# Gated attention's first pair beside the later projections, latent conditioning moved to routing and to the second attention

## The chip, the core and the metric

The kernel runs on one core of a Trainium2 chip. The metric is the device time of one execution in microseconds; lower is better. The names of the engines are those of the profile: PE is TensorE (matmuls, with PEld for its weight loads), DVE is VectorE, ACT is ScalarE, POOL is GpSimd, SP is SyncE, whose queue issues most of the DMAs.

## The reference, cut to what matters

Two transformer blocks run one after the other on 512 tokens of width 1024. The first block has 16 meta tokens in front (528 in all):

```
xn = rmsnorm(h); proj = xn @ w_in              # dq dk dv gq gk gv gr zf zb
da = diff_attention(dq, dk, dv)                # 4 heads, two softmaxes each, rope
log_g = log_sigmoid(z @ gate_w2 + b) / 16      # forward and backward gates
go = gla_bidirectional(gq, gk, gv, log_g)      # 4 heads, gated linear attention
go = rmsnorm(go) * silu(gr)
h = h + concat([da, go]) @ w_out
hn = rmsnorm(h)
h = h + peer_ffn(hn)                           # top-16 of 16384 experts, 8 heads
x = rmsnorm(h)
```

The second block is conditioned by a vector `c` (for the latents `x`) and a vector `c_ctx` (for 256 context tokens):

```
mod   = silu(c)     @ ada_w + ada_b            # 6 x 1024: sh1 sc1 g1 sh2 sc2 g2
mod_c = silu(c_ctx) @ ada_w[:, :2048] + ada_b  # only the first two
k_ctx, v_ctx = modulate(rms_norm(ctx), mod_c) @ w_in
x = x + g1 * (mix(modulate(rms_norm(x), sh1, sc1)) @ w_out)   # fourier, conv, attention
x = x + g2 * mlp(modulate(rms_norm(x), sh2, sc2))
```

## The kernel before, in words

Matrix products are made from fp32r halves: a weight tile of 128x1024 is loaded by SP (512 KB), ACT casts its high half, DVE or POOL subtracts to get the low half (`wsplit`, lines 232 to 242), and three matmuls (`mm3`, lines 220 to 223) stand for one product. The Tile scheduler puts the instructions of an engine in order: by when they are expected to be ready, and among those by their place in the program; parts inside `manual_schedule` keep the program's order.

**Projections** (lines 303 to 533). `order` lists 16 column tiles of `w_in` (0 to 3 dq, 4 to 7 dk, 8 to 11 gq and gk, 12 to 15 gr), `z` and two values `v0` (dv) and `v1` (gv). `projT`, `projz` and `projV` make them, with weights fetched four ahead into three buffers. PSUM has two double banks `psA` and four single ones `psB`; dq, gr and the values use `psB`. Postponed work (`rotate` for rope, `gate` for the gates) is held in `later` and goes out one projection later. Beside this, `ada_steps` makes the conditioning: `ada_w` is streamed as 48 rows of 128x1024, and one DVE instruction with an accumulator (line 322) multiplies a row with `silu(c)` and sums it; the first 16 rows are also summed against `silu(c_ctx)`, so there are 64 such instructions. Each projection asks for one row (`ada_go`), `projV` for two per chunk.

**Attentions** (lines 534 to 833). `gla_all` is a generator of 26 steps, 13 for each pair of heads: a diagonal, nine levels (s = 1 to 256: two exps and two masked copies on ACT, two multiplies on DVE, two adds on POOL, then the products of the level before on PE), the rest of the products, the meta rows, and at last the output matmuls with the head norm. `da_all` has 19 steps for the softmax attention. The loop at line 821 takes one gated step and about 19/22 of a softmax step at a time. Before it, an ACT table with exp and ln is loaded by hand after the last `Silu`. When the softmax steps end, three tiles of `w_out` are fetched.

**Routing** (lines 1018 to 1103) makes 16 query tiles `pq` (24 matmuls of 512 columns each), the scores, and the top 16 on DVE (`max`, `max_index`, `match_replace`); after every second tile `route` combines them. Beside it `ahead` runs passes over the expert table `u` (`upass`: 24 matmuls of 384 columns), one after an even and two after an odd tile, 24 in all; their low halves are made by POOL. `NR` = 29 passes lie before the **spread** stage, which starts when DVE has the gates; `NG` = 56 passes lie before the **v stage**, and their results are stored to DRAM and read back. In the v stage the first 56 steps have `v` alone, the other 72 also a `u` pass.

**Second attention** (lines 1598 to 1725). `pipe` runs 32 steps; step i makes the scores of one head and block, the transposes of step i-2 and the output of step i-3, with conv and Fourier steps aside in the first half. The output projection after it reads `mod[:, 16:]`.

```
821        for t in range(26):
822            next(gla, None)
823            while done < NDA and done * NE < NDA * (t + 1):
824                next(da, None)
```

## Time and profile before

| what | value |
|---|---|
| median of 3 runs | 2335.8 us (2331.62 to 2337.16) |
| the profiled execution | 2333.9 us, its span 2332.1 us |
| PE busy | 2237.0 us, 96% |
| DVE busy | 1729.0 us, 74% |
| ACT busy | 1006.2 us, 43% |
| POOL busy | 623.6 us, 27% |

The page gives busy times over the whole span. A share of the span mixes stages with different limits, so the view by stretches is read beside it: it gives each engine's busy time in a stage. Matmuls are pipelined and a row's mean duration is longer than the distance between two of them; where the pace matters, the start times of the timeline are used.

### The profile page before, as it was taken

What the parts mean: (1) busy time and instruction counts of PE and PEld (TensorE: products, weight loads), DVE (VectorE), ACT (ScalarE), POOL (GpSimd) and SP (SyncE); (2) the same over time, 40 slices, a digit from 0 to 9 for tenths busy, and PEclk for the clock granted to TensorE, in tenths of its full rate; (3) what the DMA queues carried; (4) which work ended last, traced back from release to release, by engine and by line L of the source; (5) the groups of instructions that cost most, each with busy time, mean ns of one, the idle gap of its engine ahead of it and who ended that gap; (6) DMA issues with size and microseconds to landing.
All of it is one profiled execution on the core that took longest, in us unless ns stands there. A gap on an engine that the chain in (4) does not pass through costs nothing.

```text
span 2332.1 us, 31023 instructions
## 1 busy us (share of the span) xinstructions
PE 2237.0 (96%) x11457; PEld 1883.3 (81%) x11457; DVE 1729.0 (74%) x3188; ACT 1006.2 (43%) x1439; POOL 623.6 (27%) x418
## 2 busy tenths in 40 slices
PE   7999898999999999999999999999998999999997
PEld 6777466899889878889999999999776777888885
DVE  8997776799999778887777887878687566433434
ACT  5337774433378733333333333333443654322322
POOL 2123213344310122223343443343372022000001
PEclk9999999999999999999999999999999999999999
DMA  7760023433267799998999998999321221322320
GB/s 248 261 224 10 1 81 137 167 128 111 93 231 286 304 346 340 339 335 314 312 333 314 316 335 311 322 329 310 110 93 66 73 80 64 125 92 82 117 82 36
DMA packets 158151, 458.00 MB, mean 196 GB/s; under 512 B 15248, under 2 KB 61968, under 8 KB 155696
## 3 DMA queue, kind: packets, MB, share of 16 engines
q1 hardware_dynamic: 120800, 319.57, 38.7%
q0 software_dynamic: 37200, 136.46, 16.9%
q8 instruction: 89, 1.46, 0.2%
q14 instruction: 62, 0.51, 0.1%
HBM read 419.80 MB, written 36.18 MB: 196 GB/s over the span
## 4 chain that ended last, share of the span: by engine, by line
PE 76%; DVE 8%; issue 2%; ACT 1%; DMA 1%; POOL 1%; DVEq 0%; SPq 0%; POOLq 0%; ACTq 0%
PE pu L221 8%; PE po L222 7%; PE po L221 7%; PE po L223 7%; PE pu L222 7%; PE pu L223 7%; PE pm L222 2%; PE pm L223 2%; PE pa L221 2%; PE pm L221 2%; PE pa L222 2%; DVE ac L1516 2%; PE pa L223 2%; PE pq L1187 2%; PE psB L221 2%
## 5 line engine op out<-in xcount | busy, mean ns | idle before, releaser
L221 PE MATMUL pu<-hn,uhi 128*128 128x384 f32 x1024 | 356.9, 348 | 1.6 <-DVE kc L932 0.9
L223 PE MATMUL pu<-hn,ulo 128*128 128x384 f32 x1024 | 347.2, 339 | 4.6 <-DVE ulo L234 2.7
L222 PE MATMUL pu<-hn,uhi 128*128 128x384 f32 x1024 | 347.5, 339 | 0.0
L221 PE MATMUL po<-vhi,ch 128*128 128x512 f32 x768 | 301.7, 393 | 4.8 <-ACT ch L1308 4.8
L222 PE MATMUL po<-vlo,ch 128*128 128x512 f32 x768 | 301.6, 393 | 0.1
L223 PE MATMUL po<-vhi,cl 128*128 128x512 f32 x768 | 299.2, 390 | 0.0
L1200 POOL DMA_INDIRECT gr<-in_u,idx x128 | 144.6, 1130 | 448.5 <-DVE aact L1205 416.7
L233 ACT CAST whi<-wraw 128x1024 fp32r<-128x1024 f32 x104 | 108.8, 1049 | 333.0 <-PE pm L222 127.8
L1297 ACT CAST vhi<-vraw 128x1024 fp32r<-128x1024 f32 x128 | 134.7, 1053 | 250.5 <-PE po L223 138.9
L234 POOL TENSOR_TENSOR wlo<-wraw,whi 128x1024 fp32r<-128x1024 f32 x52 | 131.6, 2536 | 383.6 <-ACT whi L233 330.1
L233 ACT CAST uhi<-uraw 128x1024 fp32r<-128x1024 f32 x105 | 110.1, 1048 | 270.0 <-PE pu L222 241.3
L1200 POOL DMA_INDIRECT gr<-in_v,idx x128 | 156.7, 1225 | 226.7 <-DVE acc L1214 189.1
L221 PEld LDWEIGHTS pu<-hn,uhi 128*128 128x128 f32 x1024 | 192.9, 188 | 5.6 <-ACT uhi L233 2.1
L223 PEld LDWEIGHTS pu<-hn,ulo 128*128 128x128 f32 x1024 | 192.7, 188 | 5.5 <-DVE ulo L234 3.1
L222 PEld LDWEIGHTS pu<-hn,uhi 128*128 128x128 f32 x1024 | 193.1, 189 | 3.5
L1309 DVE TENSOR_TENSOR vlo<-vraw,vhi 128x1024 fp32r<-128x1024 f32 x128 | 156.3, 1221 | 50.6 <-ACT vhi L1297 45.0
L234 DVE TENSOR_TENSOR wlo<-wraw,whi 128x1024 fp32r<-128x1024 f32 x52 | 63.6, 1222 | 161.5 <-ACT whi L233 161.2
L221 PEld LDWEIGHTS po<-vhi,ch 128*128 128x128 f32 x768 | 144.8, 189 | 33.9 <-ACT ch L1308 5.3
L223 PEld LDWEIGHTS po<-vhi,cl 128*128 128x128 f32 x768 | 144.9, 189 | 31.7 <-DVE cl L1310 0.2
L222 PEld LDWEIGHTS po<-vlo,ch 128*128 128x128 f32 x768 | 144.8, 189 | 27.7 <-DVE vlo L1309 0.6
L1214 DVE SCALAR_TENSOR_TENSOR acc<-gr,aact,acc 128x1024 f32<-128x1024 f32 x126 | 154.5, 1279 | 0.0
L1205 DVE CUSTOM_DVE_ANT_0 gr<-gr,hnat 128x1024 f32<-128x1024 f32 x128 | 152.6, 1220 | 0.0
(584 smaller groups left out, 5074.6 us busy)
## 6 DMA issues: line engine op xcount, KB each, us to landing
uraw<-in_ut SPq DMA_DIRECT2D x129, 512.0 KB
vraw<-in_v SPq DMA_DIRECT2D x128, 512.0 KB
aw<-in_ada SPq DMA_DIRECT2D x48, 512.0 KB
gt<-gd SPq DMA_DIRECT2D x42, 480.0 KB
wraw<-in_m SPq DMA_DIRECT2D x32, 512.0 KB
xraw<-in_m SPq DMA_DIRECT2D x32, 512.0 KB
gd<-gs SPq DMA_DIRECT2D x6, 2048.0 KB
sd<-ge SPq DMA_DIRECT2D x56, 192.0 KB
```

Of the source, the lines that this page charges most:

```text
L221: PE.matmul(out, lhs[0], rhs[0], start=first, stop=False)
L222: PE.matmul(out, lhs[0], rhs[1], start=False, stop=False)
L223: PE.matmul(out, lhs[1], rhs[0], start=False, stop=last)
L233: S.copy(hi, raw)
L234: eng.tensor_sub(lo, raw, hi.bitcast(F32))
L1187: PE.matmul(pv[:, q], oa[:, q0 + q], ob[:, j, q0 + q], start=j == 0, stop=j == 1)
L1200: G.indirect_dma_start(r, None, src, bass.IndirectOffsetOnAxis(ap=idx[:, j:j + 1], axis=0))
L1205: V.tensor_tensor_reduce(out=r, in0=r, in1=hnat, scale=1.0, scalar=0.0, op0=OP.mult, op1=OP.add, accum_out=aact[:, j:j + 1])
L1214: V.scalar_tensor_tensor(A, r, aact[:, j:j + 1], A, op0=OP.mult, op1=OP.add)
L1297: S.copy(wh, raw)
L1309: V.tensor_sub(wl, raw, wh.bitcast(F32))
L1516: V.scalar_tensor_tensor(ac[:, t], cv[:, t, j:j + N], w, ac[:, t], op0=OP.mult, op1=OP.add)
```

## The change: what it does

It reorders the projections so that the gated attention's inputs (`z`, 8 to 11) come first; the other 15 entries follow, and 12 of the 26 gated steps are emitted between their parts. dq, gr and the values move to `psA`; `psB` holds the gated steps and the values' meta rows. Weights have two buffers and are fetched two ahead, all low halves are made by DVE, `t1` has one buffer. `gr` gets one `Silu` at tile 15, and the table load by hand goes. Only the 16 context rows of the conditioning stay with the projections. The first 16 rows for the latents go to the routing (one per query tile), the other 32 to the second attention (one per step); `silu(c)` is computed in the routing, stored to DRAM and read again. `ahead` makes 7 passes in 4 tiles where it made 6, `NR` goes to 33 and `NG` to 60. The softmax steps are spread over 12 of the remaining 14 gated steps.

```
-    NR = 29
-    NG = 56
+    NR = 33
+    NG = 60
-    order = [0, 1, 'z', 8, 9, 10, 11, 'v1', 2, 3, 4, 5, 6, 7, 12, 13, 14, 15, 'v0']
-    NT = 18
+    order = ['z', 8, 9, 10, 11, 0, 1, 2, 3, 4, 5, 6, 7, 'v1', 12, 13, 14, 15, 'v0']
+    NT = 5
...
-            for j in range(48):
-                w = adp.tile([128, D], F32, name="aw", bufs=4)
+            for j in range(16):
+                w = adp.tile([128, D], F32, name="aw", bufs=2)
...
-                eng = G if len(srcs) % 3 == 0 and len(srcs) < 22 else V
-                ready.append(wsplit(wp, src, n, bufs=bufs, tag=tag, rbufs=bufs, eng=eng))
+                ready.append(wsplit(zp if tag == "wz" else wp, src, n, bufs=bufs, tag=tag, rbufs=bufs))
-            while len(ready) < 4:
+            while len(ready) < 2:
...
-                p = psB()
+                p = psA()[:, 0]
...
-                silu.append(S.activation(gr[:, j - 12], gr[:, j - 12], AF.Silu))
+                if j == 15:
+                    S.activation(gr, gr, AF.Silu)
...
         def projV(j, dst):
-            pp = [psB() for _ in range(4)] + [psA()[:, 0]]
+            pa = [psA() for _ in range(2)]
+            pp = [pa[t // 2][:, t % 2] for t in range(4)]
...
         gla = gla_all()
+        GS = 12
+        steps, parts = 0, 0
+        rest = 8 + 4 + 4 + 4
         for o in order[NT:]:
+            for _ in proj(o):
+                parts += 1
+                while steps < GS and steps * rest < GS * parts:
+                    next(gla)
+                    steps += 1
...
+    def ada_row(pool, j, sil, bufs):
+        w = pool.tile([128, D], F32, name="aw", bufs=bufs)
+        nc.sync.dma_start(w, a['ada'][j])
+        V.tensor_tensor_reduce(out=w, in0=w, in1=sil, scale=1.0, scalar=0.0, op0=OP.mult, op1=OP.add,
+                               accum_out=mod[:, j:j + 1])
...
-        NDA, NE = 19, 22
+        NDA, NE = 19, 12
-        with tc.issue_after(ins_of(silu[-1])):
-            table = S.preload_act_table_set("natural_log_exp_and_others")
-        for t in range(26):
+        for t in range(26 - GS):
...
+        sil = wp.tile([128, D], F32, name="sil")
+        nc.sync.dma_start(sil, bass.AP(tensor=a['cv'].tensor, offset=a['cv'].offset, ap=[[0, 128], [1, 1024]]))
+        S.activation(sil, sil, AF.Silu)
+        nc.sync.dma_start(sild, sil)
...
-            ahead(1 + j % 2)
+            ada_row(wp, j, sil, 3)
+            ahead(1 if j % 4 == 2 else 2)
             if j % 2:
                 route(j // 2)
+        ada_done(0, 16)
+        gains(0)
...
+        def cond(i):
+            if i < 32:
+                ada_row(adp, 16 + i, sil, 3)
-        pipe(32, (aside, 0), (na_scores, 0), (na_turn, 2), (na_out, 3))
+        pipe(32, (aside, 0), (na_scores, 0), (na_turn, 2), (na_out, 3), (cond, 0))
+    ada_done(16, 48)
+    gains(2)
```

`ada_done` adds the bias to a range of `mod`, `gains` makes one of the three scale vectors; both are one or two DVE instructions of a few columns.

## Rows read from the trace of the kernel before

**Rows 1.** The page, parts 1 and 5: busy time by engine; one group of instructions

```profile
PE 2237.0 (96%) x11457; PEld 1883.3 (81%) x11457; DVE 1729.0 (74%) x3188; ACT 1006.2 (43%) x1439; POOL 623.6 (27%) x418
...
L1205 DVE CUSTOM_DVE_ANT_0 gr<-gr,hnat 128x1024 f32<-128x1024 f32 x128 | 152.6, 1220 | 0.0
```

**Rows 2.** Busy time by stretch: length, PE, PEld, DVE, ACT, POOL, PEclk, DMA share, GB/s

```profile
24.70:189.50 164.80, 156.69 (x869) 128.83 (x868) 156.65 (x253) 59.91 (x79) 36.10 (x18) 0.99 0.62 217
189.50:313.00 123.50, 108.94 (x550) 71.69 (x550) 102.24 (x180) 100.74 (x198) 37.56 (x29) 0.96 0.02 5
313.00:338.00 25.00, 22.70 (x84) 12.65 (x83) 12.61 (x14) 19.78 (x35) 2.42 (x2) 1.00 0.07 23
...
418.00:441.00 23.00, 22.87 (x119) 20.36 (x120) 11.10 (x37) 9.95 (x13) 1.84 (x1) 1.00 0.69 251
441.00:615.00 174.00, 174.00 (x913) 157.13 (x912) 171.80 (x833) 55.74 (x79) 80.58 (x34) 1.00 0.34 115
...
845.00:1045.00 200.00, 200.00 (x884) 165.62 (x883) 162.21 (x291) 71.78 (x98) 43.31 (x46) 1.00 0.95 336
1045.00:1640.00 595.00, 595.00 (x2987) 541.71 (x2986) 473.47 (x629) 214.88 (x286) 236.29 (x193) 1.00 0.91 317
...
1802.00:1856.00 54.00, 51.99 (x275) 36.02 (x275) 31.30 (x70) 36.37 (x64) 0.00 (x0) 0.97 0.16 51
1856.00:1906.00 50.00, 49.47 (x356) 39.79 (x354) 33.23 (x81) 30.28 (x66) 6.28 (x3) 1.00 0.31 101
```

**Rows 3.** Timeline of PE in the projections: start us, length, what, idle before

```profile
24.66 1.02 PE L408 MATMUL psB<-raw,ropeP 128*128 128x512 f32 x2
...
59.88 0.36 PE L221 MATMUL psA<-xh,whi 128*128 128x264 f32 x1 [2.77 <-DVE km L455]
...
123.56 0.59 PE L221 MATMUL psA<-xh,whi 128*128 128x264 f32 x1 [2.85 <-ACT raw L447]
```

**Rows 4.** Timeline of SP's queue, first 60 us: start us, length, what is issued

```profile
14.56 0.43 SPq L385 DMA_DIRECT2D sil<-in_cv  x1
...
15.51 0.43 SPq L238 DMA_DIRECT2D wraw<-in_w1t  x1
```

**Rows 5.** Groups of DVE's instructions, 0 to 196 us: busy us, mean ns | idle before

```profile
L322 DVE CUSTOM_DVE_ANT_0 aw<-aw,sil 128x1024 f32<-128x1024 f32 x48 | 60.8, 1286 | 2.4 <-DMA aw<-in_ada 2.1
L322 DVE CUSTOM_DVE_ANT_0 at<-aw,sil 128x1024 f32<-128x1024 f32 x16 | 23.9, 1493 | 0.0
L234 DVE TENSOR_TENSOR wlo<-wraw,whi 128x1024 fp32r<-128x1024 f32 x16 | 19.5, 1218 | 0.3 <-ACT whi L233 0.2
```

**Rows 6.** Timeline of PE in the attentions

```profile
199.77 2.05 PE L584 MATMUL psB<-X,XK 128*128 128x128 f32 x16
...
321.62 3.62 PE L611 MATMUL psB<-X,XK 128*128 128x256 f32 x16
325.62 1.88 PE L663 MATMUL psB<-X,sm 128*16 128x512 f32 x4 [0.38 <-DVE X L656]
...
337.65 1.12 PE L720 MATMUL psB<-hsq,ones 128*128 128x512 f32 x2
```

**Rows 7.** Groups of ACT's instructions, 189 to 338 us

```profile
L632 ACT ACTIVATE XK<-X,half 128x512 f32<-128x512 f32 x32 | 22.7, 723 | 5.1 <-DVE X L626 3.3 <-PE psB L584 1.5 <-DVE X L625 0.3
...
L623 ACT ACTIVATE X<-P 128x512 f32<-128x512 f32 x15 | 9.5, 630 | 1.5 <-POOL P L628 1.5
```

**Rows 8.** Groups of DVE's instructions in the routing, 441 to 615 us

```profile
L1066 DVE TENSOR_TENSOR eq<-eq,tf 128x512 bf16<-128x512 bf16 x14 | 16.6, 1187 | 0.2
```

**Rows 9.** Groups of POOL's instructions in the routing, 441 to 615 us

```profile
L234 POOL TENSOR_TENSOR ulo<-uraw,uhi 128x1024 fp32r<-128x1024 f32 x21 | 51.4, 2449 | 55.8 <-ACT uhi L233 44.2 <-DMA wraw<-in_peerq 11.6
```

**Rows 10.** Groups of DVE's instructions in the spread stage, 655 to 790 us

```profile
L1154 DVE TENSOR_TENSOR bl<-eql,tw 128x512 f16<-128x512 f16 x22 | 8.4, 422 | 0.4
```

**Rows 11.** Timeline of PE in the second attention

```profile
1867.90 0.66 PE L1700 MATMUL psB<-ident,ne 128*128 128x128 f32 x4
...
1870.41 0.66 PE L1700 MATMUL psB<-ident,ne 128*128 128x128 f32 x4
```

More of the change, by code (lines that the diff above doesn't have):

```diff
@@ L299, in program @@
     lam = ap1.tile([128, 1], F32, name="lam")
-    mods = [ap1.tile([128, 24], F32, name=f"mod{j}") for j in range(2)]
     modcs = [ap1.tile([128, 8], F32, name=f"modc{j}") for j in range(2)]
@@ L420, in rotate @@
                 V.tensor_add(kr[:, j - 4], t1, raw)
-        later, silu = [], []
+        later = []
         def projT(j):
@@ new lines, in projV @@
+                        first, last = (k == 0, k == KT - 1) if t < 4 else (k == 2 * c, k > 2 * c)
+                        mm3(pp[t] if t < 4 else pm, (xh[:, k, tl], xl[:, k, tl]), (wh[:, o:o + 512], wl[:, o:o + 512]), first,
+                            last)
+                if c:
+                    V.scalar_tensor_tensor(dst[:META, 4], pm, rsc[:META, 4:5], dst[:META, 4], op0=OP.mult, op1=OP.add)
+                else:
+                    S.activation(dst[:META, 4], pm, AF.Copy, scale=rsc[:META, 4:5])
@@ L527, in program, with proj @@
+                if c < 3:
+                    yield
+            for t in range(4):
+                S.activation(dst[:, t], pp[t], AF.Copy, scale=rsc[:, t:t + 1])
+            yield
+        def proj(o):
+            if o in ('v0', 'v1'):
+                yield from projV(int(o[1]), (dv, gv)[int(o[1])])
             else:
                 projT(o)
-        ada_go(999)
+                yield
+        x0.close()
+        lv = zp.tile([128, 4, 64], F32, name="lv")
+        G.dma_start(lv, bass.AP(tensor=a['lamv'].tensor, offset=a['lamv'].offset, ap=[[0, 128], [64, 4], [1, 64]]))
@@ L530, in program @@
+        lp = zp.tile([128, 2, 64], F32, name="lp")
+        V.tensor_mul(lp, lv[:, 0:4:2], lv[:, 1:4:2])
+        ls = zp.tile([128, 2], F32, name="ls")
+        V.reduce_sum(ls, lp, AX.X)
+        S.activation(ls, ls, AF.Exp)
+        V.tensor_sub(lam, ls[:, 0:1], ls[:, 1:2])
+        V.tensor_scalar(lam, lam, 0.8 - 0.6, -1.0, op0=OP.add, op1=OP.mult)
+        projz()
+        rs_columns()
+        for o in order[1:NT]:
+            projT(o)
         while later:
             later.pop(0)()
-        x0.close()
@@ L533, in program @@
-        sps.close()
+        zs.close()
         gps = ExitStack()
@@ L677, in program @@
         gla = gla_all()
+        GS = 12
+        steps, parts = 0, 0
+        rest = 8 + 4 + 4 + 4
         for o in order[NT:]:
-            if o in ('v0', 'v1'):
-                projV(int(o[1]), (dv, gv)[int(o[1])])
-            else:
-                projT(o)
+            for _ in proj(o):
[3 more added lines that the diff above has]
+                    steps += 1
+        while later:
+            later.pop(0)()
+        ada_go(99)
+        sps.close()
     mod = const.tile([128, 48], F32, name="mod")
@@ L832, in program @@
             pass
-        aft.close()
     gps.close()
@@ L990, in program @@
     sd = dram.tile([NG, 128, ND], F32, name="sd")
+    sild = dram.tile([128, D], F32, name="sild")
     def ahead(m):
@@ L1598, in program @@
     sqs.close()
+    ads = ExitStack()
+    adp = ads.enter_context(tc.tile_pool(name="ada2", bufs=1, reuse_waits="tile"))
+    sil = adp.tile([128, D], F32, name="sil")
+    nc.sync.dma_start(sil, sild)
     mp = ExitStack()
```

68 lines of the change are left out of this document (22 added, 46 removed).

## The prediction

> **What bounds the kernel now.** I read the page first: PE is busy 96% of the span, DVE 74% [rows 1]. So the sum can only fall where PE idles or idles inside its busy figure, and I went to the stretches to see where that is. In the **projections** PE is busy 156.7 of 164.8 us, and DVE as well, 156.7 [rows 2]: two engines are full at once. The timeline shows what PE's few pauses are, two of them a wait of 2.8 us for a double bank that DVE or ACT has not yet emptied [rows 3]. In the **attentions** (189.5 to 338 us, 148.5 us) nothing is full: PE 88%, DVE 83%, ACT 82% up to 313, and then 25 us of tail in which the last gated steps stand almost alone [rows 2]. That is the stage with something to win. In the **routing** (441 to 615 us) PE has no pause at all and DVE is busy 171.8 of 174.0 us [rows 2]: again two full engines. In the **second attention** PE is full too, but DVE has room, 22.7 us of 54.0 in the first half and 16.8 of 50.0 in the second [rows 2].
>
> So this change moves PE work out of a stage where PE isn't full into one where it is, and DVE work out of a full stage into another full one and into one with room. I cost each move by that.
>
> **The projections (until 189.5 us now).** Removed from DVE: 48 sums of 1.29 to 1.49 us, 16 of the second kind and 32 of the first [rows 5], 16 x 1.49 + 32 x 1.29 = 65 us. Added to DVE: 8 low halves that POOL made, 8 x 1.22 = 10 us [rows 5], and the pair's multiplies. DVE is then far from full, and PE sets the stage. PE gets the pair's products: the diagonal, seven levels and s = 128 are each 16 matmuls in 2.0 us, s = 256 is 3.6 us, the meta rows 1.9 us [rows 6]: 9 x 2.0 + 3.6 + 1.9 = 23.5, I take 23 us. The start costs 5 us (estimate): now PE has two tiles behind it when x is normed at 24.7 us [rows 3], some 11 us of matmuls; then it has only `z`, half as long, because the next weights stand in SP's queue behind x, rope and `silu`'s input, where now a tile's load leaves at 15.5 us, right after that input [rows 4]. Of the waits, the two of 2.8 us go with DVE's load (-5.6 us); about 3 us come back, since dq and gr now take turns in two double banks and their emptying stands in ACT's queue between the pair's exps (bounds 0, and 12 x 2.8 = 34 us if each of the 12 tiles waited like rows 3). The two-deep weight fetch costs nothing as long as the split (1.05 us cast and 1.22 us) fits under a tile's 5.5 us of matmuls; without that cover, see the rivals. Sum: 23 + 5 - 5.6 + 3 = **+25 us**.
>
> **The attentions.** ACT is nearest to full: 100.7 + 19.8 = 120.5 us [rows 2]. A level takes 2 casts of 0.72 and 2 exps of 0.63, 2.7 us [rows 7]; 15 of the 18 levels fall into this stage, so three are already done beside the last projection. Six of pair one's levels leave, 16 us, and about a quarter more for copies out of PSUM (estimate): 120.5 - 20 = 101 us. The tail loses two of its four steps; from the meta rows to the last head norm it is 338.8 - 325.6 = 13 us [rows 6], with some 10 us of ACT. The rest, 91 us of ACT at the present 82%, is 112 us: 125 in all. If again three levels run early, 8 us of ACT less, it is 115. I take the middle, 120 us: **-28 us**. What goes between is one or two table loads on ACT now that none is loaded by hand; I count nothing for them, within the 10 us between those ends. Both stages together: **-3 us** (from -25, below, to +15).
>
> **The routing.** DVE gets 16 sums. Nearest rows: 1.49 us where POOL and DVE both work [rows 5], 1.22 us plus a short accumulator read where they hardly meet [rows 1]. I take 1.49: 24 us. Two of them fall into the 12 us that DVE idles before 441 us [rows 2], -2.6. PE gets four `u` passes. In the v stage 884 matmuls of 512 columns take 200 us, so 18 take 4.1 us; the mixed stretch holds 2987 / 42 = 71 steps in 595 us, 8.4 each [rows 2], so a pass is 4.3 us and four are 17 us. These four are not made later: the mixed stretch is four steps shorter, the stretch with `v` alone four longer. So the routing costs 24 - 2.6 = +21 us at DVE, and 17 us come back: **+5 us** after rounding for `Silu` and the small sums (bounds +1 at 1.22 us, +14 at the wait below). The rows' 16 loads are 8 MB on a DMA share of 0.34 [rows 2]; SP has nothing late behind them.
>
> What a DVE instruction with two inputs meets here: `eq` of 128x512 takes 1.19 us on average [rows 8] and an instruction of that size 0.42 us where POOL rests [rows 10], while POOL's low halves are 2.45 us each and fill 80.6 of 174 us [rows 2, 9]. That is a wait of 0.77 us on average, and with it a sum is 2.07 us: 16 x 2.07 - 2.6 - 17 = +14.
> By the Trainium skill (SBUF — State Buffer, section "SBUF: two separate sides") a DVE instruction with two SBUF inputs and a GpSimd instruction that reads SBUF take a shared port in turn, each for its whole length. By that rule every moved sum can be held for one of POOL's low halves, and the routing would come out nearer to +14 than to +5; the trace agrees that such waits exist.
>
> **The v stage.** 0: 60 steps with `v` alone instead of 56, at a DMA share of 0.95 and no pause on PE [rows 2]; gathers go 3% faster, since 172 units of cost stand where 177 stood. PE has cover as long as that share stays under 1 (bounds -2, +5).
>
> **The second attention.** 32 sums of 1.22 us and a read [rows 1], about 1.3 us; POOL is idle. In the second half a step is 2.51 us [rows 11], 20 steps in 50 us, and DVE needs 33.2 / 20 = 1.66 us of it. With 1.3 more it needs 2.96: DVE becomes the bound, by 0.45 us a step, 9 us in 20 steps without any gap. The first half has 22.7 us free, more than its 12 sums take (16 us), so two or three sums can be pulled into it, but each sum also holds up by up to 1.3 us whatever DVE should have started. I take **+10 us** (bounds: +2 if the free 39 us take nearly all 42 us, +20 if gaps stay as they are). SP's bias loads stand behind a row that waits for the sum three steps back; they have four buffers. The output projection only needs `mod` when its first tile is to be evacuated.
>
> **The sum**: -3 + 5 + 0 + 10 = +12 us on the profiled execution's 2333.9 us (2332.1 of span and 1.8 around it): **2346 us**. The median of the runs is 2335.8, 2 us above that execution, well inside what can be told apart: 0.3%, 7 us, is about what a measurement of this kernel can tell from no change.
>
> **The rivals.**
> *Faster: the attentions close up to ACT's floor.* With two generators at nearly equal pace and no second head norm in the middle, ACT could run at 93%: (101 - 8 - 10) / 0.93 + 13 = 102, -46 us, and with PE's products filling the bank waits the projections cost +20. That is -26; with +3 in the routing and +5 in the second attention, 2316 us. For it: three levels run early now. Against: ACT, DVE and PE are all above 80% and depend on each other. It decides once the stretch is under 112 us. Chance 0.22.
> *No change: DVE's free time takes the sums.* Second attention +3, routing +4, attentions -3: 2338 us. For it: DVE's 39 us. Against: the second half. Chance 0.20.
> *Much slower: weights come late.* With two buffers a cast waits for the tile before last, in an ACT queue with the exps; if half of 24 tiles wait 1.8 us, +22 on top: 2368 us. Against: 3 us of slack per tile. Chance 0.10.
> *The sums in the routing meet POOL every time* (the rule above): 16 x (1.3 + 2.45) - 2.6 - 17 = +40 instead of +5, 2381 us. For it: 2.45 us rows; against: the mean wait of 0.77. Chance 0.05.
> *The overlap does not come about*, because the pair's matmuls are queued behind the last projection: then only the moved sums count, about +15: 2349 us, inside the forecast's own range. Chance 0.03.
>
> **How the numbers follow.** The forecast has 0.40 and spans 2341 to 2360; with the last three rivals slower has 0.58, no change 0.20, faster 0.22. The range from 2318 to 2366 takes in most of the first two rivals and leaves out the far ends of the third and fourth.
>
> **What would show it.** Projections until about 215 us with matmuls of line 584 in them and DVE below 80%; the stretch from there to the first `wout` matmul about 120 us; in the routing DVE at 99% and small pauses on PE, or a pause before the spread stage; in the second attention steps near 3 us. I am wrong if the attention stretch is under 112 us, if the 32 sums leave PE's step at 2.5 us, or if pauses on line 221 in the projections sum to over 20 us.

## The result, and the profile after

The changed kernel takes 2395.7 us (median of 6 runs, 2389.7 to 2399.8), the kernel before 2336.5 us in as many runs beside them. The ratio is 1.0256, with an interval of 1.0239 to 1.0272. That is slower, as forecast, but by 59 us, where the forecast of 2346 us lies 10 us above that median, and beyond the range's end of 2366 us. The profiled execution of after has a span of 2396.7 us, against 2332.1 us: 64.6 us more. It is the longest of its six, so some 5 us of these 64.6 are scatter. All that follows accounts for the 64.6 us.

The first step is to put the gap in its place. The table takes the start times of the first and last matmuls of each stage from the timelines of PE in the two profiled executions.

| stage, us of the span | before | after | more | forecast |
|---|---|---|---|---|
| projections, until their last matmul | 189.1 | 218.7 | +29.6 | +25 |
| attentions, from there to the last head norm | 149.1 | 143.7 | -5.4 | -28 |
| from there to the first query tile | 85.1 | 92.5 | +7.4 | 0 |
| routing, spread and v stages | 1237.7 | 1244.4 | +6.7 | +5 |
| from there to the second attention | 141.0 | 141.9 | +0.9 | 0 |
| second attention | 105.3 | 130.0 | +24.7 | +10 |
| the rest | 424.8 | 425.5 | +0.7 | 0 |

Two of the terms carry the miss: the attentions gained 5 us instead of 28, and the second attention lost 25 instead of 10. A third was not in the sum at all.

The view by stretches of the kernel after answers to [rows 2] (length, PE, PEld, DVE, ACT, POOL, PEclk, DMA share, GB/s): projections, attentions (from the first softmax matmul on) and their tail, routing, second attention up to its last sum and behind it.

```profile
24.70:218.70 194.00, 188.95 (x1065) 156.71 (x1063) 138.83 (x220) 87.98 (x129) 42.73 (x29) 0.98 0.31 99
228.50:337.00 108.50, 92.45 (x406) 61.91 (x406) 69.99 (x123) 83.12 (x161) 12.74 (x11) 0.83 0.00 1
337.00:362.40 25.40, 21.29 (x48) 8.36 (x46) 8.47 (x9) 14.91 (x19) 0.00 (x0) 0.93 0.05 16
470.00:665.00 195.00, 195.00 (x1028) 177.12 (x1027) 193.62 (x839) 63.64 (x90) 91.99 (x37) 1.00 0.47 163
1841.00:1912.00 71.00, 49.12 (x246) 33.82 (x246) 55.87 (x114) 28.66 (x53) 0.00 (x0) 0.83 0.69 223
1912.00:1971.00 59.00, 56.34 (x392) 44.63 (x392) 38.31 (x89) 33.22 (x72) 6.77 (x3) 0.99 0.32 101
```

Read it against [rows 2]. In the projections DVE is relieved as foreseen: 138.8 of 194.0 us, 72%, where it was 95%. In the attentions no engine got fuller. All three fell: ACT is busy 77% up to 337 us where it was 82%, DVE 65% where it was 83%, and PE's granted clock is 0.83 of full speed on average. The stage now waits more than before. And the second attention has a hole: PE is busy 49.1 of 71.0 us in the first stretch, with the clock at 0.83.

The timeline of PE at the second attention's start shows the hole, and that of DVE what it waits for (start us, length, what, in brackets the idle time before and what ended it).

```profile
1841.94 0.28 PE L223 MATMUL psB<-ks,ql 64*128 64x256 f32 x1
1861.94 2.08 PE L1660 MATMUL psB<-csq,ones 128*128 128x512 f32 x2 [19.73 <-ACT csq L1656]
```

```profile
1829.84 1.21 DVE L721 CUSTOM_DVE_ANT_0 aw<-aw,sil 128x1024 f32<-128x1024 f32 x1
...
1842.21 1.23 DVE L721 CUSTOM_DVE_ANT_0 aw<-aw,sil 128x1024 f32<-128x1024 f32 x1 [1.26 <-DMA aw<-in_ada]
...
1859.39 1.23 DVE L721 CUSTOM_DVE_ANT_0 aw<-aw,sil 128x1024 f32<-128x1024 f32 x1 [0.36 <-DMA aw<-in_ada]
...
1860.54 1.28 DVE L1652 SCALAR_TENSOR_TENSOR ac<-psB,ac 128x512 f32<-128x512 f32 x2
```

The convolution's subtraction (line 1652) had its input at about 1841.3 us, when PE's matmul of line 1650 ended. But 17 of the 32 sums stand ahead of it in DVE's queue, 10 of them after that time, one in 1.9 us, since most of them wait for their row's DMA. PE waits 19.7 us for the square that ACT makes of the subtraction's result, and the scores behind it in PE's queue wait too.

The third place is the first query tile, in ACT's timeline and PE's:

```profile
443.28 1.05 ACT L233 CAST uhi<-uraw 128x1024 fp32r<-128x1024 f32 x1
451.53 1.28 ACT L1049 ACT_TABLE_LOAD   x1 [7.20 <-DMA sil<-in_cv]
452.82 1.06 ACT L1049 ACTIVATE sil<-sil 128x1024 f32<-128x1024 f32 x1
453.78 1.03 ACT L233 CAST whi<-wraw 128x1024 fp32r<-128x1024 f32 x1
```

```profile
454.87 0.80 PE L221 MATMUL pq<-hn,whi 128*128 128x512 f32 x1 [3.92 <-ACT whi L233]
```

The moved `Silu` stands in ACT's queue ahead of the first weights' cast, and its input lands late: ACT waits 7.2 us and PE 3.9 us. Another 2.5 us of this place are no loss: 43 matmuls of `u` passes stand between the last head norm and the first query tile, where the kernel before has 29, and those 14 are work drawn ahead of the mark. So some 5 of the 7.4 us are lost here, and the routing's +6.7 is nearer to 9.

### The profile page after: what moved, and what is told of

The parts are those of the page before. It is cut to its first block, busy times and chain, and to the rows that moved or that the text cites. A ratio compares the mean times of both kernels' runs of the same rounds, so it can differ in the third digit from the quotient of the medians.

```text
span 2396.7 us, 31103 instructions
## 1 busy us (share of the span) xinstructions
PE 2259.1 (94%) x11457; PEld 1898.9 (79%) x11457; DVE 1739.3 (73%) x3198; ACT 1014.6 (42%) x1443; POOL 612.9 (26%) x414
## 4 chain that ended last, share of the span: by engine, by line
PE 83%; DVE 7%; ACT 3%; DMA 3%; issue 2%; POOL 1%; DVEq 0%; SPq 0%; POOLq 0%; ACTq 0%
PE pu L221 8%; PE pu L223 7%; PE pu L222 7%; PE po L222 7%; PE po L221 7%; PE po L223 7%; PE pm L222 2%; PE pm L223 2%; PE pa L221 2%; PE pa L222 2%; PE pm L221 2%; PE pa L223 2%; PE psA L221 2%; DVE ac L1544 2%; PE psA L222 2%
## 5 line engine op out<-in xcount | busy, mean ns | idle before, releaser
L1228 POOL DMA_INDIRECT gr<-in_u,idx x128 | 144.2, 1126 | 445.0 <-DVE aact L1233 414.2
L234 DVE TENSOR_TENSOR wlo<-wraw,whi 128x1024 fp32r<-128x1024 f32 x60 | 74.8, 1247 | 166.6 <-ACT whi L233 166.1
L234 POOL TENSOR_TENSOR wlo<-wraw,whi 128x1024 fp32r<-128x1024 f32 x44 | 109.1, 2485 | 310.1 <-ACT whi L233 266.0
```

What stands on the lines that cost most here:

```text
L234: eng.tensor_sub(lo, raw, hi.bitcast(F32))
L1228: G.indirect_dma_start(r, None, src, bass.IndirectOffsetOnAxis(ap=idx[:, j:j + 1], axis=0))
```

## The experiments

The durations by stage come from the same marks as in the table above. Where code is unchanged they vary between traces: the attentions of the kernel before take 149 to 152 us in four traces, those of after 142 to 146 us in six, and after's second attention, where nothing in it was edited, some 128 to 132 us in eleven. Times are medians taken beside the kernel before, whose own median lies between 2333.5 and 2337.2 us from batch to batch. A few us between two runs are therefore less sure than a stage's change with a cause in its rows.

### The second attention: load or order?

**e2_no_sums**, the 32 rows left out.

```
-            if i < 32:
-                ada_row(adp, 16 + i, sil, 3)
+            if i == 0:
+                V.memset(mod[:, 16:48], 0.0)
```

> The changed kernel without the second attention's 32 rows and sums: the columns 16 to 47 of the conditioning are set to zero. Its time tells what that part costs in all. Queue theory: 23 to 26 us less, about 2371, hardly less than with the sums late (the first run). Load theory: the same 23 to 26 us here, but 20 us more than the first run gains.

Measured: 2370.4 us, 25.4 less than after; the stage takes 105.2 us, as before the change. So 25 us is the whole price of these 32 sums in this stage (130.0 - 105.2 = 24.8), and no other part of the change shows in it.

**e1_sums_late**, the order alone.

```
+                st_['c'] = V.scalar_tensor_tensor(ac[:, t], p, -1.0 / 256, ac[:, t], ...)
-                ada_row(adp, 16 + i, sil, 3)
+                with tc.issue_after(getattr(st_['c'], 'ins', st_['c'])):
+                    ada_row(adp, 16 + i, sil, 3)
```

> The changed kernel with one order added: the 32 sums of the second attention stand behind the convolution's subtraction (line 1652) in DVE's queue. Queue theory: of the second attention's +24.8 us nearly 20 are PE's one pause of 19.7 us at line 1660, made by 20 sums that stand ahead of that subtraction. It goes, and the run is 18 to 22 us shorter than the changed kernel, about 2376. Load theory (as the prediction had it): 32 sums of 1.3 us cost what DVE has to give, wherever they stand. Then the run is within 5 us of the changed kernel, about 2393, and the second attention's steps become longer than 2.46 us.

Measured: 2386.1 us, 9.7 less, between the two theories; the stage takes 121.6 us. (The trace counts 17 sums ahead of line 1652, not the 20 named there.) The pause at line 1660 is gone, 0.5 us instead of 19.7, but two thirds of the price stayed. A second cause that neither theory had shows in this run's timelines, of POOL, of DVE and of PE in turn:

```profile
1903.34 5.65 POOL L234 TENSOR_TENSOR wlo<-wraw,whi 128x1024 fp32r<-128x1024 f32 x2 [83.00 <-ACT whi L233]
```

```profile
1904.06 2.73 DVE L721 CUSTOM_DVE_ANT_0 aw<-aw,sil 128x1024 f32<-128x1024 f32 x1
1906.72 0.08 DVE L721 DVE_READ_ACCUMULATOR2_ANT mod<- 128x1 f32 x1
1906.72 2.55 DVE L1725 TENSOR_SCALAR ne<-ne,nz 128x512 f32<-128x512 f32 x1
```

```profile
1909.33 1.11 PE L1732 MATMUL psB<-ident,ne 128*128 128x128 f32 x4 [3.73 <-DVE ne L1725]
```

POOL makes two low halves of the next stage's weights here. Beside them a sum takes 2.73 us instead of 1.2 and a scaling of 128x512 takes 2.55 us instead of 0.48. PE pauses 3.7 us, and its granted clock is 0.50, the lower of its two levels (1.2 GHz), in the 10 us after that.

**e8_seven_ahead**, seven of the sums ahead of the stage.

```
+        for i in range(7):
+            ada_row(adp, 16 + i, sil, 3)
         cg, fg = conv(), fourier()
...
-            if i < 32:
+            if i < 25:
```

(besides, the rest behind line 1652 as in e1_sums_late)

> The changed kernel with 7 of the 32 sums ahead of the second attention, where DVE waits for the convolution's first matmul, and 25 behind line 1652. If what the first run left (16 of 25 us) is DVE's load with sums in every step, 25 instead of 32 take back 7 x 1.3 = 9 us against the first run: about 2377. If it is the 5.6 us of POOL's low halves that met DVE there (one sum 2.7 us, one scaling 2.6 us) and the lower clock behind that pause, the gain depends on whether they meet again: about 2376 if not, and 2386 if so.

Measured: 2383.9 us, 2.2 less than with all late, where 9 were forecast for load alone; the stage takes 118.5 us, 3.1 less. The meeting with POOL is there again (a sum of 2.74 us at 1905.61 us, a scaling of 2.55 us behind it). That leads to the next run.

**e13_low_halves_dve**, as e8_seven_ahead, with those two low halves made by DVE.

```
-            w = wsplit(wp, a['wout2'][d], bufs=2, eng=G if d < 7 else V)
+            w = wsplit(wp, a['wout2'][d], bufs=2, eng=G if 2 <= d < 7 else V)
```

> The run with seven sums ahead (2383.9 us), and besides, the first two low halves of the output projection's weights, which POOL made at 1905 us beside a sum and a scaling of 2.5 us and more, are made by DVE (2 x 1.22 us). If that meeting costs the pause of some 3 us and the stretch at the lower clock behind it: 5 to 8 us less, about 2377. If DVE's load is what is left: 0 to +3, since DVE gets 2.4 us more.

Measured: 2376.7 us, 7.2 less than e8_seven_ahead (4.6 less when each is set against the kernel before of its own batch), and the stage takes 113.0 us, 5.5 less, though DVE has more to do. The meeting cost that. What is left of the 24.7 us is 113.0 - 105.3 = 7.7 us, with 25 sums still in the stage. It goes with DVE's load and was not split further. So of the stage's price 8.4 us went with the order in the queue, 5.5 with the meeting that this order led to, and 3.1 with the seven sums that stand ahead of the stage.

### The overlap: does it pay?

**e3_no_overlap**, no early gated steps.

```
-        GS = 12
+        GS = 0
-        NDA, NE = 19, 12
+        NDA, NE = 19, 22
```

> The changed kernel with the gated attention's 12 early steps put back behind the projections (12 becomes 0, and the softmax steps are spread over 22 gated ones as in the kernel before); order of the tiles, buffers and the moved conditioning stay. Theory that the softmax part paces the attentions whether 14 or 26 gated steps stand beside it: the projections end 23 us earlier, near 196, the attentions take about 150 us, and the last head norm ends near 346: 16 us less, about 2380. Theory that the overlap does what it is for and something else (order, buffers) costs the 24 us: the attentions grow by the 23 us that the projections lose, or by more, and the run is within 5 us of the changed kernel or slower.

Measured: 2388.2 us, 7.5 less than after (5.6 less, each set against the kernel before of its batch), between the two. The projections end at 199.7 us (19.0 earlier) and the attentions take 157.0 us (13.3 more). The overlap therefore loses 5.7 us. But the run shows more: without any overlap the two stages are still 18.5 us longer than before the change, 10.6 in the projections and 7.9 in the attentions. That remainder belongs to other parts of the edit.

**e15_six_early**, half of the overlap.

```
-        GS = 12
+        GS = 6
-        NDA, NE = 19, 12
+        NDA, NE = 19, 17
```

> The changed kernel with 6 early gated steps instead of 12, and the softmax steps spread over 17 of the 20 left. Theory that each early step costs PE its matmuls in the projections and gives less back, since the softmax steps alone need some 113 us: between the runs with 12 and with none, about 2391. Theory that the first few early steps pay (they stand where the projections have gaps of ACT and DVE, and enough gated steps stay to lie beside the softmax steps): under 2386.

Measured: 2391.5 us, as the first theory has it: projections until 209.0, attentions 149.2 us. Neither six nor twelve early steps pay.

**e4_gated_first**, the order inside the stage.

```
-            while done < NDA and done * NE < NDA * (t + 1):
+            while done < NDA and done * NE < NDA * (t - 3):
```

(and 10 instead of 12 for `NE`)

> The changed kernel with the softmax steps emitted only from the fifth remaining gated step on (the second pair's diagonal and first levels go first). Theory that the stage loses time because softmax steps run alone for its first 35 us: the second pair's levels then start near 231 instead of 264 and stand beside softmax steps, and the stage is 8 to 15 us shorter, about 2385. Theory that the 16 softmax steps themselves are the chain that sets the stage: they start some 12 us later, and the run is 5 to 12 us longer, about 2404.

Measured: 2406.9 us, 11.2 more. That is the second theory's number, but not its place. The gated steps do come early, and the last softmax output ends 9.2 us later (350.6 us instead of 341.4), but this comes out of the gated tail behind it: the stage takes 144.2 us, as in after. The 11.6 us that are lost stand behind the last head norm, where PE waits for the first tile of `w_out`, which is fetched when the softmax steps end:

```profile
374.39 0.79 PE L221 MATMUL psA<-mix,whi 128*128 128x512 f32 x1 [10.79 <-ACT whi L233]
```

So this run doesn't show that the softmax steps alone set the stage's end. In after the last softmax output ends at 341.4 us, and 21 us of gated steps follow it.

### What the softmax steps wait for

**e5_softmax_alone** and **e6_gated_alone** leave out one side each.

```
-            for hp in range(2):
+            for hp in range(1):
```

```
-                if t < 16:
-                    da_scores(t)
-                if 2 <= t < 18:
-                    da_turn(t - 2)
-                if t >= 3:
-                    da_out(t - 3)
                 yield
```

> The changed kernel without the second gated pair (its two heads are set to zero): in the attentions only the first pair's end and the 16 softmax steps are left. Read is the stretch from the last projection matmul to the last head norm's matmul, 143.7 us in the changed kernel. Theory that the softmax steps are a chain of their own (scores, maximum, exponential, over two double banks): the stretch stays at 105 us or more, some 6 us a step, though ACT has only about 70 us of work in it. Theory that ACT's work sets the stage: without the second pair the stretch falls to about 85 us.

> The changed kernel without the softmax attention (its four tiles are set to zero): in the attentions only the first pair's end and the second pair are left. Same stretch. Chain theory: 35 to 45 us, so that the two alone add up to within 10 us of the 143.7 us that they take together. ACT theory: 45 to 60 us, and the sum of the two is no measure of the whole.

Both stretches, of the one kernel and then of the other (columns as in the view by stretches):

```profile
221.60:334.30 112.70, 94.08 (x282) 51.34 (x280) 52.59 (x99) 65.89 (x128) 1.84 (x2) 0.76 0.03 9
```

```profile
218.10:282.00 63.90, 53.48 (x251) 35.04 (x249) 34.17 (x39) 39.41 (x63) 19.95 (x13) 1.00 0.12 36
```

The softmax attention alone takes 112.7 us with ACT busy 65.9 and DVE 52.6: it is not ACT's work, as the first theory says. The gated pair alone takes 63.9 us, more than either theory had, so the two do overlap: 112.7 + 63.9 is 33 us more than the 143.7 us together. Both stretches begin with the first pair's end, 10 us, which this sum counts twice, so some 23 of the second pair's 54 us hide beside the softmax steps. With the second pair gone 78% of the stage is left.

Is it one chain of waits? The first stretch has a granted clock of 0.76 on the mean. In it two lots of three tiles each can be compared, with the same matmuls and no gated work beside them, between the starts of the tiles' first scores (tiles 4 to 6 and 8 to 10; columns as above):

```profile
249.22:263.75 14.53, 14.53 (x39) 8.93 (x40) 7.39 (x17) 7.75 (x18) 0.00 (x0) 0.50 0.00 0
272.18:280.97 8.79, 7.83 (x40) 4.88 (x39) 5.17 (x11) 6.89 (x16) 0.00 (x0) 1.00 0.01 2
```

At the lower level of PE's clock (0.50, 1.2 GHz) PE has no pause and a tile takes 4.8 us; at the upper one (2.4 GHz) it takes 2.9 us. So part of the 112.7 us is PE at half its clock, 1.9 us a tile, and not the length of the chain. After's stage has a mean clock of 0.86, some 41 us at the lower level; the kernel before, with gated matmuls between the tiles, has 0.97, some 10 us. By the ratio of the two rows 31 us more at the lower level cost up to 12 us. That is an estimate, and an upper one, since PE pauses in part of that time; no run takes the clock away alone.

**e9_scores_twice**, each score matmul issued twice.

```
-                    PE.matmul(p[:, hf, :264], qz[cs, h, ...], kr[cs, h, ...],
+                    for _ in range(2):
+                        PE.matmul(p[:, hf, :264], qz[cs, h, ...], kr[cs, h, ...],
```

> The changed kernel with every score matmul of the softmax attention issued twice (same operands, same result): 128 more matmuls of 264 columns, some 28 us of PE at the upper level of its clock, more at the lower. Clock theory: the softmax steps are long because PE, left without the gated pair's matmuls, is granted only 0.50 of its clock from 236 to 262 us and again near 305 and 315; with twice the scores it is granted more, and the attention stretch (143.7 us) stays within 8 us. Latency theory: each step is a chain PE, DVE, ACT that is long at any clock, and the scores stand in it; the stretch grows by 16 to 28 us.

Measured: 2422.6 us, 26.9 more, and the attentions take 169.6 us, 25.9 more. The group of the score matmuls, of after and of this run (busy us, mean ns of one | idle before, ended by):

```profile
L786 PE MATMUL psA<-kr,qz 64*128 64x264 f32 x128 | 39.5, 507 | 11.1 <-ACT e L790 11.1
```

```profile
L787 PE MATMUL psA<-kr,qz 64*128 64x264 f32 x256 | 66.5, 488 | 8.1 <-ACT e L791 8.1
```

Of PE's extra 27.0 us, 25.9 arrive in the stage, although PE idles in it. So the scores stand in the chain, as the latency theory says. The granted clock rose between 238 and 258 us, from 0.50 to 0.67, and fell elsewhere; over the stretch it is 0.84, where after has 0.86. So this run does not part the clock from the chain; the two rows of e5_softmax_alone above do.

**e10_scale_later** and, on the kernel before, **e12_before_scale_later** take the scaling out of the way of the next tile.

```
+        def da_norm(i):
+            pc, Z = ds.pop(('p', i))
             r = dp.tile([128, 2], F32, name="rZ", bufs=4)
...
+                if 1 <= t < 17:
+                    da_norm(t - 1)
```

> The changed kernel with the softmax steps cut in two: reciprocal, scaling on ACT and the subtraction on DVE of one tile are emitted one step later, behind the next tile's scores. If a step is long because the next tile's maximum and exponentials queue behind this tile's scaling on DVE and ACT, a step falls from some 6.5 to under 5.5 us and the attentions get 10 to 16 us shorter, about 2383. If the two double banks (scores, maximum and exponential of one half, then the next scores) are what it waits for, nothing changes: within 4 us of 2396.

> The kernel before with the softmax steps cut in two as in the run on the changed kernel. If there the cut shortens the attentions, it does so here by half as much at most, since 22 gated steps stand beside the softmax steps and cover them: 0 to 6 us less, about 2333. If it does nothing there, nothing here.

Measured: 2397.2 us, no change, and 1.0005 of the kernel before (0.9996 to 1.0014), no change either. The place of the scaling in the queues of ACT and DVE is not what a step waits for. The row above, of the whole stage, says what PE waits for ahead of the scores: the exponential that empties their double bank, 11.1 us. A third double bank was not tried, since all of PSUM is taken; that the two banks set the step is therefore argued, not shown.

### The table loads

Something in the edit costs the attentions 5 to 8 us with no overlap at all. The groups of ACT's instructions from 60 to 380 us show what was taken away, here of before and then of after, table loads only:

```profile
L487 ACT ACT_TABLE_LOAD x1 | 1.3, 1283 | 0.0
...
L460 ACT ACT_TABLE_LOAD x1 | 1.3, 1283 | 0.0
...
L818 ACT ACT_TABLE_LOAD x1 | 1.3, 1283 | 0.0
```

```profile
L750 ACT ACT_TABLE_LOAD x4 | 5.1, 1283 | 0.1
...
L751 ACT ACT_TABLE_LOAD x4 | 5.1, 1283 | 0.1
...
L630 ACT ACT_TABLE_LOAD x2 | 2.6, 1283 | 0.1
...
L486 ACT ACT_TABLE_LOAD x1 | 1.3, 1283 | 0.0
...
L459 ACT ACT_TABLE_LOAD x1 | 1.3, 1283 | 0.0
```

Lines 750 and 751 are the logarithm and the exponential of a head norm. The kernel before loaded by hand (line 818) one table that has both.

**e17_table_by_hand** puts that load back.

```
-                    S.activation(gr, gr, AF.Silu)
+                    silu.append(S.activation(gr, gr, AF.Silu))
...
+        with tc.issue_after(ins_of(silu[-1])):
+            table = S.preload_act_table_set("natural_log_exp_and_others")
+        aft = ExitStack()
+        aft.enter_context(tc.issue_after(ins_of(table)))
         for t in range(26 - GS):
```

> The changed kernel with the hand-made ACT table load of the kernel before (one load behind the gates' Silu, all ACT work of the attentions behind it). It spares 8 or 9 table loads of 1.28 us, two in each head norm, 10 to 11 us of ACT. Theory that a head norm's loads hold up the softmax exponentials behind them in ACT's queue and, at the end, the last head norm itself: 6 to 11 us less, about 2388. Theory that ACT has room for them, since the softmax chain waits for its double banks: within 3 us of 2396.

Measured: 2381.2 us, 14.5 less than after, more than the first theory's 11. The attentions take 133.3 us, 10.4 less, as this run's view by stretches has it (ACT 91.0 us where after has 100.3):

```profile
218.20:351.50 133.30, 119.40 (x474) 72.11 (x473) 79.03 (x133) 91.04 (x177) 12.76 (x11) 0.88 0.02 5
```

Seven of the eight loads lie in the stage, 9.0 us of ACT; the eighth begins at 363.7 us, right behind its last mark. So the loads count about one for one, in a stage in which ACT is busy 70% of the time. The other 4 us of the 14.5 lie mostly in stages that this edit doesn't touch. In after's timeline of ACT a head norm's two loads stand ahead of the exponentials for which the softmax steps wait:

```profile
228.32 0.63 ACT L748 ACTIVATE hsq<-ho 128x512 f32<-128x512 f32 x1
228.96 1.28 ACT L750 ACT_TABLE_LOAD   x1
230.26 1.26 ACT L750 ACTIVATE hr<-psB,c 128x512 f32<-128x512 f32 x2
231.54 1.28 ACT L751 ACT_TABLE_LOAD   x1
232.84 1.06 ACT L751 ACTIVATE hr<-hr 128x1024 f32<-128x1024 f32 x1
233.80 0.68 ACT L790 ACTIVATE e<-psA,nm 128x528 f32<-128x528 f32 x1
```

### The start, and the conditioning alone

**e14_tile_first**: tile 0 ahead of `z`.

```
-    order = ['z', 8, 9, 10, 11, 0, 1, ...
+    order = [0, 'z', 8, 9, 10, 11, 1, ...
-    NT = 5
+    NT = 6
...
+        projT(0)
         x0.close()
```

(tile 0 in a single bank; a second fetch after the fifth part of x)

> The changed kernel with one query tile of 512 columns put ahead of the gates' tile, its weights fetched first and its bank a single one, as the kernel before has it. Theory that the late start (PE's first matmul at 20.2 us instead of 7.5) is the order alone: the tile's 24 matmuls, 5.5 us, run before 20 us, and the projections end 5 to 8 us earlier, about 2389. Theory that the start is bound by x's loads and DVE, or that the gates and so the first pair's steps come later by as much: within 3 us of 2396.

Measured: 2389.2 us, 6.5 less (3.5 less, each set against the kernel before of its batch). PE's first matmul moves from 20.2 to 9.5 us, where the cast of its own weights ends:

```profile
9.52 0.79 PE L221 MATMUL psB<-xh,whi 128*128 128x512 f32 x1 [9.52 <-ACT whi L233]
```

PE is busy 8.6 us before 20 us, but the projections end only 3.5 us earlier. From 20 to 30 us the granted clock is 0.69, where after has 1.00. The order is thus part of the late start; the rest was not followed.

**e7_conditioning_only**: the kernel before, with only the conditioning moved.

```
-            for j in range(48):
+            for j in range(16):
...
+            ada_row(wp, j, sil, 3)
-            ahead(1 + j % 2)
+            ahead(1 if j % 4 == 2 else 2)
...
-        pipe(32, (aside, 0), (na_scores, 0), (na_turn, 2), (na_out, 3))
+        pipe(32, (aside, 0), (na_scores, 0), (na_turn, 2), (na_out, 3), (cond, 0))
```

(and 33 and 60 for `NR` and `NG`)

> The kernel before with only the conditioning moved (16 rows stay beside the projections, 16 sums in the routing, 32 in the second attention; 33 and 60 for the two block counts); projections and attentions as before. My theory: routing and v stage cost +5 to +7, the second attention +25 as in the changed kernel, and DVE's relief gives back at most the 10 us of PE's pauses in the projections: 20 to 28 us over the kernel before, about 2358. Rival: the relief of 48 sums on a DVE that is full gives the projections 20 us or more, and the run is under 2348; then the attention half alone costs nearly all of the 59 us.

Measured: 2364.9 us, 1.0118 of the kernel before (1.0101 to 1.0135), 28.7 us more, just past the upper edge of my 20 to 28. The projections end at 183.5 us, 5.6 earlier, routing to v stage +4.3, the second attention 129.6 us, +24.3, and the stretch up to the first query tile +4.2, of which 2.5 us are the `u` pass's matmuls drawn ahead and 1.2 PE's wait behind the late `Silu`. So the conditioning accounts for some 29 of the 59 us, and the attention half for the rest, if the two add.

**e11_before_eight_rows**: the kernel before, 8 of its rows moved to where DVE idles ahead of the second attention.

```
-            for j in range(48):
+            for j in range(40):
...
+        for c in range(40, 48):
+            aw = adp.tile([128, D], F32, name="aw", bufs=3)
+            nc.sync.dma_start(aw, a['ada'][c])
+            V.tensor_tensor_reduce(out=aw, in0=aw, in1=sil, ..., accum_out=mod[:, c:c + 1])
         cg, fg = conv(), fourier()
```

> The kernel before with only the last 8 of its 32 conditioning rows that the second block needs moved, to the start of the second attention, where DVE idles 11 us ahead of the convolution. Theory that the move costs nothing as far as it fills that idle time, and that DVE's load in the projections is worth about a third of itself (7 us of start and bank waits came back in the run with the conditioning alone, for 62 us of sums): projections 1 to 4 us shorter, second attention 0 to +3: within 3 us of the kernel before, 2334. Theory that any sum in the second attention costs its 1.3 us there: +8 us, 2343.

Measured: 2339.7 us, 1.0017 of the kernel before (1.0008 to 1.0025): 3.7 us more, of which 2.3 us lie in the second attention. The price is below 1.3 us a sum, but nothing is won: DVE's relief in the projections is worth 0.7 us here. The kernel before isn't beaten by it.

### The repairs together

**e16_three_repairs** is e13_low_halves_dve with e14_tile_first and e3_no_overlap; **e18_four_repairs** has the table load by hand too.

> The changed kernel with no early gated steps, the query tile first, seven sums ahead, the others behind line 1652 and the two low halves on DVE. If the parts add up: 2396 less 8 (no overlap), less 6 (start), less 18 (second attention): 2364, some 28 us over the kernel before, of which 6 are the routing, some 8 the second attention's load and the rest the tiles' order and buffers. If DVE's queue or the start's weights make them work against each other: 2375 or more.

> The run with three repairs (2374.7 us) and the hand-made table load. Without the overlap the trace shows 11 table loads of 1.28 us in the attentions, 14 us. If they are the 8 to 11 us by which its attentions (160.2 us) are longer than those of the kernel before (149.1 us): 8 to 12 us less, about 2365. If the tiles' order or the buffers are: within 3 us of 2374.

Measured: 2374.7 us for three. They do not add up: without the overlap the tile in front brings nothing (projections until 200.2 us), and the attentions take 160.2 us. With the table load the time is 2352.3 us, 22.4 less (18.2 between the two profiled executions), more than the 14 us of loads that go: the projections end at 192.8 us instead of 200.2, the attentions take 151.4 us, as in the kernel before (149 to 152), the second attention, which this edit doesn't touch, 112.4. In the projections PE's waits for the copies out of its double banks (ACT, lines 441 and 445) fall from 8.9 to 2.5 us. With the table's place fixed, the first exps of the gated pair (lines 631 and 632) start at 168.5 us, behind the last `Silu`, and no longer at 72.1 us, between those copies.

The best of all versions of the change is thus 1.0064 of the kernel before (1.0046 to 1.0082). It has the conditioning moved and no overlap. No version run here beats the kernel before.

## Why the prediction was wrong

The sign was right, with the chance of 0.58 on its side, and most of the places were right. The size failed in two terms and for want of a third. By the prediction's steps:

**Projections, +25: 29.6 measured.** The pair's products, 23 us by rows, cost 19.0 (e3_no_overlap), or 25.4 between the two runs with the table by hand (218.2 and 192.8 us), which differ in the start too. DVE's relief, -5.6 us, is just what e7_conditioning_only gives. (The 48 sums that left are those of 1.29 us: 62 us and not 65. The term does not use it.) The 3 us of waits for the double banks did not come; PE waited 4.2 us once for the pair's own `XK`. Too small was the start, "5 us (estimate)": I saw that `z` is a short tile with late weights behind it, but put PE's lack of work too low. PE's first matmul comes at 20.2 us in after's timeline, where 11.7 us of matmuls lie ahead of 20 us in the kernel before (2.5 in its first 10 us, 9.2 in the next):

```profile
20.21 2.13 PE L371 MATMUL psA<-sqa,ones 128*128 128x264 f32 x4 [20.21 <-DVE sqa L368]
```

By e3_no_overlap the products cost 4 us less than forecast, and what is left over (29.6 - 19.0 + 5.6 = 16 us of start and waits) twice the 8 forecast, so the near hit of this term is in part luck. The rival of late weights did not occur; PE waits for no cast in the projections of after.

**Attentions, -28: -5.4 measured.** This is the step that failed: "The rest, 91 us of ACT at the present 82%, is 112 us", with 13 us of tail behind it and the middle taken with a shorter case, 120 in all. The two parts of the stage in after, parted at the second pair's meta rows:

```profile
218.70:343.75 125.05, 108.52 (x442) 68.41 (x440) 70.73 (x124) 88.30 (x169) 12.74 (x11) 0.85 0.02 5
343.75:362.40 18.65, 15.01 (x34) 6.07 (x33) 8.47 (x9) 12.02 (x16) 0.00 (x0) 0.91 0.07 22
```

So the rest took 125 us and not 112, the tail 19 and not 13, and nothing came of the shorter case. The amount of ACT was not too small: 100.3 us of work in the stage with the table loads and 91.0 without, where 101 were forecast. The share was wrong, 71% in place of 82%. ACT doesn't set the pace: the softmax steps take 113 us with no second pair beside them and ACT 58% busy (e5_softmax_alone, five table loads among them), in part because PE falls to its lower clock when the gated matmuls are gone. The prediction has no term for the clock. In [rows 2] ACT, DVE and PE were all over 80% busy, since much gated work filled the gaps between the softmax steps. Filler taken away lowers the share (ACT from 81% of the whole stage, 120.7 of 149.1 us, to 70%) more than the time. The faster rival, closing up to ACT's floor, falls with it.

The second half of the miss is a sentence: "one or two table loads on ACT now that none is loaded by hand; I count nothing for them". There are eight, seven of them in the stage, and with them gone it is 10.4 us shorter. The removed line stood in the diff, each head norm uses a logarithm and an exponential, and the kernel before shows a load of 1.28 us. The term could have been worked out: 4 head norms times 2 loads. How the remaining 12 us or so part between the clock and the waits of the softmax steps stays open.

**Between the stages: 0 forecast, +7.4 measured.** Of `Silu` in the routing I counted no wait. It made PE wait 3.9 us here and 1.2 us in e7_conditioning_only; 2.5 us are a `u` pass drawn ahead of the mark. The rest, some 1 us, was not followed.

**Routing, +5: +6.7 measured.** Here the steps held singly. Up to the v stage it is +26.1, where 21 were forecast, the v stage -19.4, where 17 were. A sum takes 1.60 us on average, near the 1.49 taken, and between the bounds of 1.22 and 2.07; that each one meets POOL, the rival of 40 us, did not come about. (POOL's low halves fill 51.4 us of the routing [rows 9]; the 80.6 us that I gave them are all of POOL's work there.) By the rule of the Trainium skill (SBUF — State Buffer, "SBUF: two separate sides") each sum could have been held for a whole low half. In after's routing three of the sixteen took 3.1 to 3.2 us and the others 1.2 to 1.5, so few were, and the 2.73 us in the second attention of e1_sums_late show one more.

**Second attention, +10: +24.7 measured.** The load term was good: "DVE becomes the bound, by 0.45 us a step, 9 us", and 7.7 us is what remains with the order repaired and 25 of the sums in the stage. What I had not followed is what the scheduler does with 32 instructions that are ready early. I did write that each sum "holds up by up to 1.3 us whatever DVE should have started", but gave it room only inside the bound of +20. In after 17 of them stand ahead of the one DVE instruction on which PE's whole queue depends, and those after 1841 us come at one in 1.9 us. Of my own signs, "if the 32 sums leave PE's step at 2.5 us" came true: the last 18 steps take 46.0 us before and after (from the 14th to the last `reduce_max` of line 1721), since all sums are done by 1907 us.

The rivals with 42% of the chance fell with these steps: the faster one needed ACT's share to hold and rise, and no change needed the sums for next to nothing, where 7.7 us stayed even with their order mended and seven of them outside.

## What to carry to other kernels

A stage in which several engines are 80% busy may still be paced by steps that wait for each other, with filler in their gaps. Before taking filler out, time those steps alone: a run with one side left out tells in one profile what the stage can fall to, and its clock column tells whether PE keeps its upper level without the filler. When a diff takes out a hand-made table load, count the functions that alternate behind it. And work with no due time of its own, put into an in-order queue, needs an order: tie it behind the first instruction that others wait for.

## What the runs showed of the hardware that was not expected

A table load costs its 1283 ns on the way to the next exponential and little beside: between the rows at 228.96 and 230.26 us above lie 1.30 us. With seven of them, 9.0 us, gone from it, the stage was 10.4 us shorter. The Trainium skill (ScalarE: Activation LUTs, "What ACT_TABLE_LOAD costs") has the same 1283 ns but counts 2.66 us for a switch, with a drain of 1.38 us. No drain of that size shows in this trace: the instruction ahead ends at 228.95 us, 0.01 us before the load begins. The measurement decides.

A DVE scaling with one SBUF input (128x512, `L1725`) was held up by POOL's low halves as much as a sum with two: 2.55 us instead of 0.48.

PE lost its upper clock level in the attentions: 0.50 granted (1.2 GHz) between 239 and 259 us, when the gated matmuls had left, where in the kernel before no 10 us of the stage showed less than 0.83. The table load's gain is apart from it: e17_table_by_hand has 20 such us at 0.50 and 0.51. A softmax tile with nothing beside it took 4.8 us at the lower level and 2.9 us at the upper one (e5_softmax_alone).
